# A hybrid encoder step on one core: W_out prepared by ScalarE and GpSimd, the last head pair's mask added by TensorE, its cached keys stacked one step sooner

## The chip, the core and the metric

The kernel runs on one core of a Trainium2 chip. The core has five instruction streams that matter here: TensorE (PE in the profile, with its weight loads shown apart as PEld), VectorE (DVE), ScalarE (ACT), GpSimd (POOL) and SyncE (SP), which only issues DMA transfers. Each stream runs its instructions in order; streams wait for one another by semaphores. The metric is the device time of one execution in microseconds.

## The reference, cut to what matters

The reference computes one layer of an encoder for a prompt of 1024 frames and for a sample of 64 further frames, whose 512 earlier frames lie in a cache. A combined projection of x feeds three groups of heads: six forgetting-attention heads (fox), four channel groups of a spatial-gating MLP (sgu), and six stick-breaking heads (sb). The head outputs are normalised per head, multiplied by a gain `g_mix`, and go through one output projection `w_out`; then come a layer norm, an MLP of 4096 hidden columns and a second layer norm.

What the change touches is the stick-breaking attention and the gain with the output projection:

```python
z = jnp.einsum('bqhd,bkhd->bhqk', q, k).astype(jnp.float32) / math.sqrt(D_HEAD)
mask = kpos[None, :] < qpos[:, None]
log_rem = jnp.where(mask, jax.nn.log_sigmoid(-z), 0.0)
after = lax.cumsum(log_rem, axis=3, reverse=True) - log_rem
a = jnp.where(mask, jnp.exp(jax.nn.log_sigmoid(z) + after), 0.0)
...
oh = oh * lax.rsqrt(jnp.mean(oh * oh, axis=-1, keepdims=True) + RMS_EPS)
o = (oh.reshape(B, T, D_MIX) * g_mix).astype(o_sgu.dtype)
return jnp.einsum('bte,ed->btd', o, w_out)
```

The kernel takes the weight of a key as sigmoid(z) times the product of sigmoid(-z) over the keys between it and the query.

## The kernel before

**Numbers in two parts.** A matrix operand is kept as a rounded high part (type fp32r) and the rest, its low part. ACT makes the high part with a copy that rounds; a subtraction (`lo_sub`, L97) makes the low part on DVE or POOL. A product is three matmuls, high by high, high by low, low by high (`PASSES`).

**The stage with the change.** Two generators are traced in turns by a loop with hand-set costs: `fill` (projections) and `attn` (attention). `attn` runs over six head pairs (three fox, then sb 0, 1, 2; the last is `pairs[5]`). For each pair it takes four steps u of 256 queries, each for two heads h, and then the sample. A step is `Unit.a_steps` (scores and weights) and `Unit.b_steps` (transposes of the weights, their split in two parts, the product with the values). `fill` meanwhile makes the next pair's keys, values and queries; beside the last pair it makes the gate `u` of the sgu group (`sgu_u`), and then the first two tiles of the output projection (`mix`, L244). A scheduler under the kernel fixes each engine's order from readiness in its own model and the order of the trace, so that an instruction can run well ahead of its place in the program.

- **Scores** (`qk_rows`, L554): into a PSUM bank of tag s, of which there are two. On the diagonal block of 128 keys DVE adds the mask `m_fox` or `m_sb` (L561, 128 x 128). For sb two sigmoids on ACT follow (L536, L537), a scan of products on DVE from the last key to the first (L538, up to 1024 columns), and a product on POOL (L540). PE transposes the result (L602, ptsb), ACT and DVE split it (L570 and L97, pthsb), PE multiplies by the values (L612 to L615, osb), ACT copies the result out (L625, osbsb), PE transposes it into the one bank of tag tr (L633, otpsb), and DVE adds up two halves (L634).
- **The sample's cache** (`Sample`): `load` at u = 1 fetches keys and values by DMA; `prep_steps`, traced at u = 3, transposes the keys in two rounds through the tr bank (L671, pkcsb), and `k_stack` copies each head's part on ACT (L441) and takes the low part on DVE (L97), both into kc_sb; POOL makes the values' parts (L676, L97, vc_sb). `a_steps` then multiplies (L692, Ss0sb). The two kc tiles are of tag kp, which has ten buffers; the pair's four key tiles and the five partial sums `up` of `sgu_u` have the same tag.
- **W_out** (`load_wo`, sixteen calls of 128 x 512, named xT<-rwo in the profile): a DMA (L970) puts a piece into a raw tile (tag vp, ten buffers, or raw, two). ACT writes piece x gain, rounded, into the high part (L973), and DVE writes piece x gain - high into the low part (L974). The parts lie in the memory of `xT`, the transposed input, so that each piece waits until the projections have read that part of xT. `sgu_u` calls them from its tile 4 on.
- **sgu_u** (L355, sgu<-wu,xT): for nine tiles and two halves of the depth, into one of two acc banks. The first half is copied out by ACT (L853, up), the second added by DVE (L856), then the gelu goes over ACT, DVE (L752), ACT and POOL (L754), and a DMA stores it to u_dr.
- **mix**: `prep` loads a tile of head outputs (oo, from o_dr) and of u_dr (uu), POOL multiplies (L183), ACT squares (L185), DVE sums and scales (L187, L192); the tile is transposed (L200) and split (oTb), and 48 matmuls (L244, mx) follow.

The SP queue issues all these DMAs in one order: raw pieces of weights, query copies (L115), stores to o_dr and u_dr, loads of oo and uu.

Of the kernel before, what the change touches and what calls it, by code (L numbers as in the profile page):

```python
# [12 lines left out]
F32 = mybir.dt.float32  # L13
F32R = mybir.dt.float32r
AF = mybir.ActivationFunctionType
ALU = mybir.AluOpType
# [4 lines left out]
P = 128  # L21
# [15 lines left out]
BIG = 1e30  # L37
# [19 lines left out]
def _build(nc, tc, a, es):  # L57
# [23 lines left out]
    ident = cp.tile([P, P], F32, name="ident")  # L81
# [14 lines left out]
    def lo_sub(eng, out, src, hi):  # L96
        eng.tensor_tensor(out, src, hi.bitcast(F32), op=ALU.subtract)  # L97
# [22 lines left out]
    wo = []  # L120
# [161 lines left out]
    gmx = sp.tile([P, KT], F32, name="gmx")  # L282
    with ExitStack() as p1:
        sa = p1.enter_context(tc.tile_pool(name="sa", bufs=1, side="right"))
# [4 lines left out]
        def mask(name, base, fill):  # L289
            m = sp.tile([P, P], F32, name=name + "_f", tag="gl", bufs=3)  # L290
            nc.gpsimd.memset(m, 0.0)
            nc.gpsimd.affine_select(m, m, pattern=[[-1, P]], compare_op=ALU.is_ge,
                                    fill=fill, base=base, channel_multiplier=1)
            r = sp.tile([P, P], F32R, name=name)
            nc.vector.tensor_copy(r, m)
            return r

        m_fox = mask("m_fox", 0, BIG)
        m_sb = mask("m_sb", -1, -BIG)

# [239 lines left out]
            nc.gpsimd.tensor_tensor(s[:, 0:n - 1], s[:, 0:n - 1], g[:, 1:n], op=ALU.mult)  # L540
            return s

        def qk_rows(nm, qd, h, half, nk, kp, msk):
            chunks = []
            eng = {"dve": nc.vector, "pool": nc.gpsimd, "pe": nc.tensor}['dve' if msk is m_fox else 'dve']
            on_pe = eng is nc.tensor
            for c0 in range(0, nk, 512):
                w = min(512, nk - c0)
                sps = ps.tile([P, 512], F32, name=f"S{nm}_{c0}", tag="s", bufs=2)
                for b0 in range(c0, c0 + w, 256):  # L550
                    n = min(256, nk - b0)
                    last = b0 + n == nk
                    for s in range(2):
                        nc.tensor.matmul(sps[:, b0 - c0:b0 - c0 + n], qd[:, h, s, half * P:(half + 1) * P],  # L554
                                         kp[b0 // 256][:, h, 0:n], start=(s == 0), stop=(s == 1 and not (last and on_pe)))
                    if last and on_pe:
                        nc.tensor.matmul(sps[:, w - P:w], identr, msk, start=False, stop=True)
                    elif last:
                        d = sps[:, w - P:w]
                        if eng is nc.vector:  # L560
                            nc.vector.tensor_tensor(d, d, msk.bitcast(F32), op=ALU.add)  # L561
                        else:
                            nc.gpsimd.affine_select(d, d, pattern=[[-1, P]], compare_op=ALU.is_ge,
                                                    fill=BIG if msk is m_fox else -BIG,
                                                    base=0 if msk is m_fox else -1, channel_multiplier=1)
                chunks.append((c0, w, sps[:, 0:w]))
            return chunks

# [4 lines left out]
        class Unit:  # L573
# [4 lines left out]
            def a_steps(self):  # L578
                st, u, h = self.st, self.u, self.h
                for half in range(2):  # L580
                    i = 2 * u + half
                    nk = (i + 1) * P
                    k2 = f"{st['nm']}_{i}_{h}"
                    ch = qk_rows(k2, st["qd"][u], h, half, nk, st["kp"], m_fox if st["fox"] else m_sb)
                    if st["fox"]:
                        hh = 2 * st["hp"] + h
                        self.rows.append(softmax_rows(k2, ch, st["cb"][h], nk, lsum[:, i, hh:hh + 1]))
                    else:
                        self.rows.append(stick_rows(k2, ch, nk))
                    yield 0.109 * (i + 2)  # L590
# [281 lines left out]
        pairs = []  # L872
        for fox, hp in ((True, 2), (True, 1), (True, 0), (False, 0), (False, 1), (False, 2)):
# [3 lines left out]
                fox=fox, hp=hp, first=first, quick=len(pairs) in (0, 1, 5), nm=pre + str(hp), nv=262 if first else 256,  # L877
                scale=-0.125 if fox else 0.125, qd={}, kp=[], vp=[],
# [85 lines left out]
        def load_wo(i, half, q):  # L964

            k = 4 * i + q
            cs = slice(half * 512, (half + 1) * 512)
            raw = (sa.tile([P, 512], F32, name=f"rwo{k}_{half}", tag="vp", bufs=10) if (2 * k + half) % 3
                   else sp.tile([P, 512], F32, name=f"rwo{k}_{half}", tag="raw", bufs=2))
            nc.sync.dma_start(raw, w_out[:, k, cs])  # L970
            hi = wo[i][0][:, q, cs]
            g = gmx[:, k:k + 1]
            nc.scalar.activation(hi, raw, AF.Copy, scale=g)  # L973
            nc.vector.scalar_tensor_tensor(wo[i][1][:, q, cs], raw, g, hi.bitcast(F32),  # L974
                                           op0=ALU.mult, op1=ALU.subtract)

        cur = {"j": 0}

        def attn():
            seq = []  # L980
            for j, st in enumerate(pairs):
                for u in range(4):
                    for h in range(2):
                        seq.append((j, u, h, Unit(st, u, h)))
                seq.append((j, 4, 0, Sample(st)))

            def a_of(x):
                j, u, h, un = x
                cur["j"] = j
                st = pairs[j]  # L990
                if u < 4:
                    if u == 0 and h == 0:
                        if j == 5:
                            yield (5, "kv")
                        st["smp"] = seq[[i for i, y in enumerate(seq) if y[0] == j and y[1] == 4][0]][3]
                    yield (j, u)
                    if u == 0 and h == 0:
                        if j == 0:
                            yield (0, "c0")
                        if st["fox"]:  # L1000
                            st["cb"] = []
                            for hh in range(2):
                                cb = sp.tile([P, TP], F32, name=f"cb{st['nm']}_{hh}", tag="row", bufs=ROWS)
                                r = 2 * st["hp"] + hh
                                nc.sync.dma_start(cb, bcast(c_dr[r:r + 1, 0:TP]))
                                st["cb"].append(cb)
                    if u == 1 and h == 0:
                        st["smp"].load()
                    if u == 3 and h == 0:
                        yield from st["smp"].prep_steps()  # L1010
                if j == 0 and u == 4:
                    yield (0, "c1")
                yield from un.a_steps()
                if u < 4 and h == 1:
                    live["qd"] -= 1

            settled = set()

            def settle(x):
                c_pend.extend(c_list)  # L1020
                c_list.clear()
                if x[:3] in settled:
                    return
                settled.add(x[:3])
                if x[1] == 3 and x[2] == 1:
                    live["kp"] -= 4
                if x[1] == 4:
                    live["kn"] -= 1

            nxt = a_of(seq[0])  # L1030
            yield from nxt
            for i, x in enumerate(seq):
                b = x[3].b_steps()
                nxt = a_of(seq[i + 1]) if i + 1 < len(seq) else iter(())
                alive = [nxt, b]
                k = 0
                while alive:
                    g = alive[k % len(alive)]
                    try:
                        c = next(g)  # L1040
                    except StopIteration:
                        alive.remove(g)
                        continue
                    if isinstance(c, tuple) and c not in done:
                        for cb_ in b:
                            yield cb_
                        settle(x)
                    yield c
                    k += 1
                    if k == 2 and c_pend:  # L1050
                        while c_pend:
                            c_pend.pop(0)()
                settle(x)
            while c_pend:
                c_pend.pop(0)()
# [392 lines left out]
    with p3:  # L1448
# [100 lines left out]
        with in_order(border):  # L1549
            raw = up_load(2)  # L1550
            ch = chain(1, 0)
# [25 lines left out]
        ch = chain(NP - 3, 1)  # L1577
        for i in range(7):
            ch.product(i)
        ch = chain(NP - 3, 0)  # L1580
# [82 lines left out]
    with ExitStack() as p3:  # L1663
# [290 lines left out]
        g = 2 * c  # L1954
# [135 lines left out]
```

## Time and profile before

| | |
|---|---|
| runs shown | 1410.02, 1411.81, 1411.91 us; median 1411.81 |
| the profiled execution's own time | 1411.73 us |
| its span, first to last instruction | 1410.0 us |
| granted TensorE clock, mean | 0.980 |
| PE busy | 1328.1 us, 8827 matmuls |
| DVE, ACT, POOL busy | 1002.6, 718.5, 602.3 us |

The page of the profile has the busy time of each engine, the span in 40 slices with the busy share of each engine in tenths, the chain that ended last, and groups of equal instructions. A group's row gives line, engine, operation, the tile written and those read with shapes, then busy time, mean duration in ns, and the idle time of its engine just before with what ended it. A row of the waits says who waited for whom: total us, times, longest. A row of the order in time gives start, duration, engine, line and operation. A row of stretches gives the stretch, its length, the busy time of each engine with its instructions, the granted clock, the share of DMA and its GB/s; asked for one line alone it shows that line's engine only.

### The profile page before, as it was taken

How to read it: one execution, taken by the hardware profiler on the slowest of the kernel's cores; microseconds unless marked ns; L12 is line 12 of the kernel's file. 1: busy time of each engine (PE TensorE's matmuls, PEld its weight loads, DVE VectorE, ACT ScalarE, POOL GpSimd, SP SyncE). 2: the span in 40 equal slices, each digit the busy share in tenths (PEclk: the TensorE clock that was granted, in tenths of full speed). 3: DMA queues.
4: the chain of work that ended last, by engine and by line, in shares of the span. 5: the costliest groups of instructions: out<-in, count | busy, mean ns of one | idle time of the engine just before them, and what ended most of it. 6: DMA issues, size and time to landing. Idle time of an engine off the chain costs nothing.

```text
span 1410.0 us, 24288 instructions
## 1 busy us (share of the span) xinstructions
PE 1328.1 (94%) x8827; PEld 1206.8 (86%) x8827; DVE 1002.6 (71%) x1799; ACT 718.5 (51%) x1561; POOL 602.3 (43%) x663
## 2 busy tenths in 40 slices
PE   7999999999989997999989999999979999999996
PEld 6899999999888986866889999999967787777774
DVE  3577565676786599887866768767678777667777
ACT  3366565666665485333423323232247667667675
POOL 3222222266565535654411122212166665654657
PEclk9999999999999998999999999999999999999999
DMA  7324242322313434422234434344558344344343
GB/s 218 77 78 113 58 117 65 81 63 56 80 27 83 127 91 135 132 105 68 76 110 140 153 133 139 117 166 139 173 187 295 99 160 165 118 136 150 101 135 128
DMA packets 149217, 168.87 MB, mean 120 GB/s; under 512 B 27100, under 2 KB 115484, under 8 KB 149096
## 3 DMA queue, kind: packets, MB, share of 16 engines
q1 hardware_dynamic: 149096, 167.30, 37.9%
q8 instruction: 70, 1.15, 0.3%
q14 instruction: 51, 0.42, 0.1%
HBM read 109.26 MB, written 51.71 MB: 114 GB/s over the span
## 4 chain that ended last, share of the span: by engine, by line
PE 63%; DVE 12%; ACT 7%; DMA 6%; POOL 6%; issue 5%; SPq 1%; DVEq 0%; ACTq 0%; POOLq 0%
PE zA L1264 9%; PE A L1715 6%; PE zD L1264 6%; PE mx L244 5%; PE kvsb L355 5%; PE kvfox L355 4%; PE D L1715 3%; PE zC L1264 3%; PE zB L1264 3%; DVE snsb L538 2%; DMA raw<-w_in 2%; PE qfox L496 2%; PE Sfox L554 2%; DMA rd<-w_down 2%; PE ptfox L602 1%
## 5 line engine op out<-in xcount | busy, mean ns | idle before, releaser
L97 POOL TENSOR_TENSOR wa<-wr,wa 128x512 fp32r<-128x512 f32 x42 | 63.8, 1548 | 228.5 <-ACT wa L1204 228.5
L97 POOL TENSOR_TENSOR wd<-rd,wd 128x512 fp32r<-128x512 f32 x77 | 101.1, 1322 | 121.2 <-ACT wd L1204 116.9
L244 PE MATMUL mx<-xT,oTb 128*128 128x512 f32 (+1 forms) x416 | 108.0, 412 | 1.6 <-ACT oTb L202 1.5
L1264 PE MATMUL zD<-xo,ws 128*128 128x288 f32 (+1 forms) x720 | 98.1, 289 | 0.6 <-DVE h4a L1426 0.3
L1264 PE MATMUL zA<-xo,ws 128*128 128x288 f32 (+1 forms) x720 | 98.1, 290 | 0.0
L244 PEld LDWEIGHTS mx<-xT,oTb 128*128 128x128 f32 (+1 forms) x416 | 78.1, 193 | 21.7 <-ACT oTb L202 2.5
L1264 PEld LDWEIGHTS zD<-xo,ws 128*128 128x128 f32 x720 | 93.7, 189 | 1.1 <-DVE h4a L1426 0.5
L1264 PEld LDWEIGHTS zA<-xo,ws 128*128 128x128 f32 x720 | 94.1, 189 | 0.1
L540 POOL TENSOR_TENSOR sgsb<-sgsb,snsb 128x127 f32<-128x127 f32 (+7 forms) x48 | 58.8, 1227 | 78.8 <-DVE snsb L538 64.3
L355 PE MATMUL kvfox<-wkvfox,xT 128*128 128x256 f32 (+3 forms) x624 | 90.6, 294 | 1.5 <-ACT wkvfox L331 0.5
L1204 ACT ACTIVATE wd<-rd 128x512 fp32r<-128x512 f32 x105 | 63.8, 624 | 51.6 <-DMA rd<-w_down 25.8
L355 PE MATMUL kvsb<-wkvsb,xT 128*128 128x256 f32 (+1 forms) x624 | 87.7, 286 | 0.0
L1715 PE MATMUL A<-wd,wd 128*128 128x512 f32 x312 | 83.0, 401 | 2.5 <-DVE acc L1682 2.3
L355 PEld LDWEIGHTS kvfox<-wkvfox,xT 128*128 128x128 f32 (+1 forms) x624 | 81.6, 193 | 3.3 <-DVE xT L97 1.0
L1396 POOL TENSOR_TENSOR rd<-rd 128x512 f32<-128x512 f32 x56 | 78.9, 1409 | 10.9 <-DVE b L97 8.7
L538 DVE TENSOR_TENSOR_SCAN snsb<-snsb,one 128x128 f32<-128x128 f32 (+7 forms) x48 | 72.2, 1507 | 13.3 <-ACT snsb L537 12.5
L1275 ACT ACTIVATE sn<-zA 128x256 f32<-128x256 f32 (+1 forms) x80 | 31.0, 390 | 98.4 <-PE zA L1264 82.6
L355 PEld LDWEIGHTS kvsb<-wkvsb,xT 128*128 128x128 f32 (+1 forms) x624 | 79.2, 187 | 0.2
L1715 PEld LDWEIGHTS A<-wd,wd 128*128 128x128 f32 x312 | 58.9, 191 | 18.9 <-DVE acc L1682 4.2
L1715 PE MATMUL A<-wd,h4a 128*128 128x512 f32 x240 | 65.1, 395 | 0.4 <-DVE acc L1682 0.3
L1478 ACT ACTIVATE ws<-wr 128x1024 fp32r<-128x1024 f32 x28 | 29.0, 1057 | 54.0 <-DVE wr L1214 54.0
L1715 PEld LDWEIGHTS A<-wd,h4a 128*128 128x128 f32 x240 | 44.5, 188 | 12.6 <-ACT p L1732 1.2
(537 smaller groups left out, 3746.2 us busy)
## 6 DMA issues: line engine op xcount, KB each, us to landing
h_dr<-hh SPq DMA_DIRECT2D x30, 512.0 KB, 3.2
rd<-w_down SPq DMA_DIRECT2D x30, 512.0 KB, 4.5
awa<-h_dr SPq DMA_DIRECT2D x30, 512.0 KB, 4.5
wr<-w_up SPq DMA_DIRECT2D x14, 1024.0 KB, 5.4
hr<-h_dr SPq DMA_DIRECT2D x32, 384.0 KB, 3.6
h_dr<-hh SPq DMA_DIRECT2D x30, 384.0 KB, 3.9
raw<-w_in SPq DMA_DIRECT2D x44, 256.0 KB, 3.3
xr<-x_prompt SPq DMA_DIRECT2D x8, 512.0 KB, 7.2
```

Source lines behind the costliest of these rows:

```text
L97: eng.tensor_tensor(out, src, hi.bitcast(F32), op=ALU.subtract)
L244: nc.tensor.matmul(acc[0:m], oT[:, k, hx, 0:m], wo[k // 4][hw][:, k % 4, cs], start=(i == 0), stop=(i == len(seq) - 1))
L355: nc.tensor.matmul(acc[0:n, c0:c0 + n1 - n0], xT[k // 4][:, k % 4, c:c + n], wt[:, k, hw, n0:n1], start=(i == 0), stop=(i == len(seq) - 1))
L496: nc.tensor.matmul(acc[:, 0:w], wq[:, k, hw, :], xT[k // 4][:, k % 4, c:c + w], start=(i == 0), stop=(i == len(seq) - 1))
L538: nc.vector.tensor_tensor_scan(g[:, 0:n][:, ::-1], g[:, 0:n][:, ::-1], one.broadcast_to([P, n]), 1.0, op0=ALU.mult, op1=ALU.bypass)
L540: nc.gpsimd.tensor_tensor(s[:, 0:n - 1], s[:, 0:n - 1], g[:, 1:n], op=ALU.mult)
L1204: nc.scalar.activation(hi, raw, AF.Copy)
L1264: nc.tensor.matmul(z, w[:, hw, k], xop(s, bo, hx)[:, k, :], start=(new and k == 0 and j == 0), stop=(k == 3 and j == 2), skip_group_check= ...
L1275: nc.scalar.activation(c, z, AF.Copy)
L1396: eng.tensor_tensor(r[:, o], r[:, x], r[:, y], op=ALU.subtract)
L1478: nc.scalar.activation(ws[:, 0, q, c], src[:, q], AF.Copy)
L1715: nc.tensor.matmul(z, h[:, hx, q, o], wset[self.c % 2][q][:, hw, wb], start=((n in (0, 3) or n == 1 and self.c == 0) and q == 0 and j == 0 ...
```

## The change

It has three parts and one helper tile. (1) `load_wo`: the gain is multiplied into the raw tile in place by ACT, a second ACT copy rounds it into the high part, and POOL makes the low part with `lo_sub`; DVE has no part in it. (2) `qk_rows` has an argument `on_pe`, set for the last pair alone: there the mask is added in PSUM by a further matmul, of a rounded identity `identr` with the mask, and DVE does not touch the scores. `identr` is made by one DVE copy at the start. (3) The sample's `prep_steps` of the last pair (j = 5) is traced at u = 2 instead of u = 3. Code that no path used goes with it.

```diff
--- before.py
+++ after.py
@@ -295,6 +295,8 @@
             nc.vector.tensor_copy(r, m)
             return r
 
+        identr = sa.tile([P, P], F32R, name="identr")
+        nc.vector.tensor_copy(identr, ident)
         m_fox = mask("m_fox", 0, BIG)
         m_sb = mask("m_sb", -1, -BIG)
 
@@ -540,10 +542,8 @@
             nc.gpsimd.tensor_tensor(s[:, 0:n - 1], s[:, 0:n - 1], g[:, 1:n], op=ALU.mult)
             return s
 
-        def qk_rows(nm, qd, h, half, nk, kp, msk):
+        def qk_rows(nm, qd, h, half, nk, kp, msk, on_pe=False):
             chunks = []
-            eng = {"dve": nc.vector, "pool": nc.gpsimd, "pe": nc.tensor}['dve' if msk is m_fox else 'dve']
-            on_pe = eng is nc.tensor
             for c0 in range(0, nk, 512):
                 w = min(512, nk - c0)
                 sps = ps.tile([P, 512], F32, name=f"S{nm}_{c0}", tag="s", bufs=2)
@@ -557,12 +557,7 @@
                         nc.tensor.matmul(sps[:, w - P:w], identr, msk, start=False, stop=True)
                     elif last:
                         d = sps[:, w - P:w]
-                        if eng is nc.vector:
-                            nc.vector.tensor_tensor(d, d, msk.bitcast(F32), op=ALU.add)
-                        else:
-                            nc.gpsimd.affine_select(d, d, pattern=[[-1, P]], compare_op=ALU.is_ge,
-                                                    fill=BIG if msk is m_fox else -BIG,
-                                                    base=0 if msk is m_fox else -1, channel_multiplier=1)
+                        nc.vector.tensor_tensor(d, d, msk.bitcast(F32), op=ALU.add)
                 chunks.append((c0, w, sps[:, 0:w]))
             return chunks
 
@@ -581,7 +576,8 @@
                     i = 2 * u + half
                     nk = (i + 1) * P
                     k2 = f"{st['nm']}_{i}_{h}"
-                    ch = qk_rows(k2, st["qd"][u], h, half, nk, st["kp"], m_fox if st["fox"] else m_sb)
+                    ch = qk_rows(k2, st["qd"][u], h, half, nk, st["kp"], m_fox if st["fox"] else m_sb,
+                                 st is pairs[5])
                     if st["fox"]:
                         hh = 2 * st["hp"] + h
                         self.rows.append(softmax_rows(k2, ch, st["cb"][h], nk, lsum[:, i, hh:hh + 1]))
@@ -969,10 +965,9 @@
                    else sp.tile([P, 512], F32, name=f"rwo{k}_{half}", tag="raw", bufs=2))
             nc.sync.dma_start(raw, w_out[:, k, cs])
             hi = wo[i][0][:, q, cs]
-            g = gmx[:, k:k + 1]
-            nc.scalar.activation(hi, raw, AF.Copy, scale=g)
-            nc.vector.scalar_tensor_tensor(wo[i][1][:, q, cs], raw, g, hi.bitcast(F32),
-                                           op0=ALU.mult, op1=ALU.subtract)
+            nc.scalar.activation(raw, raw, AF.Copy, scale=gmx[:, k:k + 1])
+            nc.scalar.activation(hi, raw, AF.Copy)
+            lo_sub(nc.gpsimd, wo[i][1][:, q, cs], raw, hi)
 
         cur = {"j": 0}
 
@@ -1006,7 +1001,7 @@
                                 st["cb"].append(cb)
                     if u == 1 and h == 0:
                         st["smp"].load()
-                    if u == 3 and h == 0:
+                    if u == (2 if j == 5 else 3) and h == 0:
                         yield from st["smp"].prep_steps()
                 if j == 0 and u == 4:
                     yield (0, "c1")
```

## The prediction

> **What bounds the kernel now.** The page first: which engine is full, and where.
>
> ```profile
> span 1410.0 us, 24288 instructions
> ...
> PE 1328.1 (94%) x8827; PEld 1206.8 (86%) x8827; DVE 1002.6 (71%) x1799; ACT 718.5 (51%) x1561; POOL 602.3 (43%) x663
> ...
> PE   7999999999989997999989999999979999999996
> ...
> DVE  3577565676786599887866768767678777667777
> ```
>
> PE is the bound over the whole, so only time in which PE stands still can be won. A slice is 35.25 us; in the 15th and 16th (493 to 564 us) DVE is at 9 tenths, and in the 16th PE falls to 7. The edits lie there, from the last stick-breaking pair's scores (477 us) to the first output-projection matmul (558.5 us). The table by stretches:
>
> ```profile
> 477.00:558.50 81.50, 68.74 (x518) 65.55 (x516) 74.76 (x114) 57.97 (x142) 40.37 (x42) 0.94 0.42 126
> ...
> 500.00:558.50 58.50, 48.06 (x354) 45.73 (x353) 55.28 (x79) 40.84 (x95) 25.95 (x23) 0.91 0.38 117
> ...
> 560.00:580.00 20.00, 19.64 (x104) 16.11 (x103) 17.39 (x36) 7.06 (x15) 16.25 (x17) 1.00 0.39 126
> 580.00:600.00 20.00, 20.00 (x94) 16.16 (x93) 13.95 (x23) 6.38 (x10) 12.12 (x13) 1.00 0.46 140
> 600.00:616.00 16.00, 16.00 (x79) 12.41 (x78) 11.90 (x20) 5.78 (x10) 7.17 (x12) 1.00 0.27 99
> ```
>
> Columns: stretch, length, busy PE, PEld, DVE, ACT, POOL, then granted clock. In 477 to 558.5 PE idles 81.50 - 68.74 = 12.8 us while DVE is busy 74.76 of 81.5; from 500 on DVE is at 94.5% and the clock is 0.91, a further 48.06 x 0.09 = 4.3 us. From 560 to 616 PE is full, so what is won before 558.5 arrives at the end unless something later waits on a fixed time, and I see nothing such. Who holds PE there, by the waits (total us, times, longest):
>
> ```profile
> PE Ss0sb L692 <- DVE kc_sb L97: 3.7, 1, 3.7
> PE osb L614 <- DVE pthsb L97: 3.4, 3, 1.8
> PE Ssb L554 <- ACT snsb L537: 1.9, 2, 1.6
> ...
> ACT sgsb L536 <- DVE Ssb L561: 9.6, 6, 2.3
> ```
>
> DVE's order in time shows what stands ahead of those it keeps waiting:
>
> ```profile
> 512.09 1.40 DVE L974 SCALAR_TENSOR_TENSOR xT<-rwo,gmx,xT 128x512 fp32r<-128x512 f32 x2
> 513.41 1.27 DVE L97 TENSOR_TENSOR pthsb<-ptsb,pthsb 128x512 fp32r<-128x512 f32 x2
> ...
> 527.81 3.13 DVE L974 SCALAR_TENSOR_TENSOR xT<-rwo,gmx,xT 128x512 fp32r<-128x512 f32 x2
> 530.86 0.28 DVE L561 TENSOR_TENSOR Ssb<-Ssb,m_sb 128x128 f32<-128x128 f32 x1
> ...
> 542.30 2.21 DVE L752 SCALAR_TENSOR_TENSOR g1u<-g1u,up 128x256 f32<-128x256 f32 x1
> 544.43 1.80 DVE L974 SCALAR_TENSOR_TENSOR xT<-rwo,gmx,xT 128x512 fp32r<-128x512 f32 x2
> 546.26 0.42 DVE L97 TENSOR_TENSOR kc_sb<-pkcsb,kc_sb 64x256 fp32r<-64x256 f32 x1
> ...
> 547.05 0.75 DVE L974 SCALAR_TENSOR_TENSOR xT<-rwo,gmx,xT 128x512 fp32r<-128x512 f32 x1
> 547.71 1.15 DVE L97 TENSOR_TENSOR pthsb<-ptsb,pthsb 128x512 fp32r<-128x512 f32 x2
> ```
>
> L974 makes the low parts of W_out, which nobody needs before 558.5. Yet the split of the probabilities (pthsb) comes behind it at 512 and 547, the mask L561 at 530.9 comes behind 3.13 us of it, and the cached keys' low part (kc_sb) at 546.26. So 3.7 + 3.4 + 1.6 (the longer wait of Ssb, by way of mask and sigmoid) = **8.7 us** of PE's 12.8 idle stand behind L974, L561 or a late kc_sb.
>
> **The change, part by part.** The rows of what goes and of the nearest to what comes:
>
> ```profile
> L974 DVE SCALAR_TENSOR_TENSOR xT<-rwo,gmx,xT 128x512 fp32r<-128x512 f32 x16 | 15.5, 995 | 0.7 <-ACT xT L973 0.7
> ...
> L561 DVE TENSOR_TENSOR Ssb<-Ssb,m_sb 128x128 f32<-128x128 f32 x15 | 4.4, 294 | 3.8 <-PE Ssb L554 3.5
> ...
> L973 ACT ACTIVATE xT<-rwo,gmx 128x512 fp32r<-128x512 f32 x16 | 10.8, 731 | 0.0
> ...
> L331 ACT ACTIVATE wu<-raw 128x512 fp32r<-128x512 f32 x4 | 2.4, 624 | 0.0
> ...
> L97 POOL TENSOR_TENSOR wu<-raw,wu 128x512 fp32r<-128x512 f32 x4 | 5.2, 1294 | 0.3 <-ACT wu L331 0.3
> ...
> L554 PE MATMUL Ssb<-kpsb,qdsb 128*128 128x128 f32 x14 | 2.6, 269 | 0.3 <-ACT snsb L537 0.3
> ```
>
> Edit 1, W_out: DVE loses 16 L974, 15.5 us. ACT keeps 16 scalings at 0.73 us (now in place) and gains 16 plain copies at 0.624 = 10.0 us. POOL gains 16 subtractions at 1.294 = 20.7 us. The scaling no longer writes xT, so it need not wait until the projection has read xT. Behind each subtraction on POOL stand the stick-breaking products (L540) and the gelu products (L754), for which transposes and stores wait. The raw tile comes free after POOL instead of DVE, and the SP queue already stands for that:
>
> ```profile
> SPq L970 <- DVE xT L974: 8.6, 7, 3.7
> ...
> L970 SPq DMA_DIRECT2D rwo<-w_out x16: 327/330/537, 473.5 to 531.8; - x16
> ```
>
> The 16 loads are the same; behind a waiting one on SP stand stores to o_dr and u_dr and the loads of uu and oo for the first projection tile. I cost this at nothing: POOL has 58.5 - 25.95 = 32.6 us idle after 500. Without that cover it is a subtraction for each of the seven waits, 7 x (1.294 - 0.995) = 2.1 us.
>
> Edit 2, masks: DVE loses 16 x 0.294 = 4.7 us (15 of them in the stretch); ACT's sigmoid follows PE directly, so its 9.6 us of waiting for masks go. PE gains 16 matmuls of 128 columns in fp32r. That operation (ident by mask, whole) is not in the trace; one of 128 columns in a row of others:
>
> ```profile
> 492.47 0.22 PE L613 MATMUL osb<-pthsb,vpsb 128*128 128x128 f32 x1
> 492.53 0.28 PE L614 MATMUL osb<-pthsb,vpsb 128*128 128x128 f32 x1
> 492.64 0.33 PE L615 MATMUL osb<-pthsb,vpsb 128*128 128x256 f32 x1
> ```
>
> L613 and L614 take 0.17 us from start to start for two (0.09 each), and the 128-column form of L554 lasts 0.269 us in the mean, overlaps counted: 16 x 0.09 = 1.4 to 16 x 0.269 = 4.3 us. Nothing can be gained below zero, since it is added work. I take 0.12 us, near the first, because the mask follows two matmuls of its own group: **1.9 us**. The copy identr is one DVE cast at the start, where DVE still waits for the first x; 0.2 us without that cover.
>
> Edit 3, cache keys: four transposes, four ACT copies, four DVE subtractions move from u = 3 to u = 2, one step of the pair earlier. No DMA moves, since the load stays at u = 1, and the values' parts on POOL ran early already:
>
> ```profile
> L97 POOL TENSOR_TENSOR vc_sb<-cache_sb_v,vc_sb x12: 451/457/464, 320.9 to 477.0; 128x128 fp32r<-128x128 f32 x12
> ```
>
> The last of twelve ran at 477.0, some 70 us ahead of the key's low part at 546.26. The 3.7 us wait goes. The four keys still take the one tr bank, for which the output transposes of the finished heads wait, but one step sooner, in DVE's company of fewer instructions; I cost that at nothing. The copies may wait for a buffer (first rival).
>
> What is late next: ACT. In the stretch it rises to 57.97 + 10.0 = 68.0 us. After 500 it has 40.84 + 10.0, less the scalings of the first six tiles, which can run before 500 (six, an estimate: the buffers that tags vp and raw have free by the code): 6 x 0.73 = 4.4. That is 46.4 us of some 53, 12% free, where DVE has 5.5% free now. New waits on ACT lie between nothing and the 8.7 us that DVE causes. If waits go as the inverse of the free share, 8.7 x 5.5 / 12 = 4.0 us; counting only the 5.0 that edit 3 does not move, 2.3 us. I take **3.0**. The clock recovers with the idle time: (8.7 - 3.0) / 12.8 x 4.3 = 1.9 us.
>
> Sum: -8.7 + 3.0 + 1.9 - 1.9 = **-5.7 us**. The profiled execution took 1411.73 us, 1.73 more than its span, and the median of the runs shown is 1411.81, so the one stands for the other: 1411.7 - 5.7 = **1406.0**.
>
> [...] The trace shows POOL and DVE standing in each other's way:
>
> ```profile
> L974 DVE SCALAR_TENSOR_TENSOR xT<-rwo,gmx,xT x16: 721/740/2464, 500.3 to 547.0; 128x512 fp32r<-128x512 f32 x16
> ...
> 541.88 2.35 POOL L540 TENSOR_TENSOR sgsb<-sgsb,snsb 128x1023 f32<-128x1023 f32 x1 [2.29 <-PE sgu L355]
> ```
>
> L752 began at 542.30, within this POOL instruction, lasted 2.21 us and ended at 544.51, just after POOL at 544.23; L974 ranges from 0.72 to 2.46 us. Its 16 cost 15.5 - 16 x 0.72 = 4.0 us beyond their least. [...]
>
> ```profile
> 477.00:558.50 81.50, 25.96 (x16) 0.94 0.42 126
> ```
>
> [...]
>
> **The rivals.** (a) *Buffers for the cache keys.* Tag kp has ten: four hold the pair's keys, five the projection's partial sums (up), one is left until a sum is used up. Two key tiles taken sooner leave the ninth tile's sum without one until then.
>
> ```profile
> L853 ACT ACTIVATE up<-sgu x9: 360/391/445, 489.8 to 513.3; 128x256 f32<-128x256 f32 x8, 64x256 f32<-64x256 f32 x1
> ...
> 522.74 1.74 POOL L754 TENSOR_TENSOR sguu<-g1u,up 128x256 f32<-128x256 f32 x2
> ```
>
> It was stored at 513.3; the first sum is used up at 524.5. For 11 us one of two acc banks would be held, and some four projection tiles (an estimate) would each wait for their emptying, 0.42 us as kc_sb takes and one pthsb ahead of it on DVE, 1.27 / 2: 4 x 1.06 = 4.2 us, so **1410.2**. Against: another pair's buffers come free meanwhile. Chance 0.11. (b) *ACT becomes what DVE was*, all 8.7 us remain and the masks are added: **1413.6**. For: 12% free. Against: ACT loses its 9.6 us of waiting. 0.05. (c) *Edit 3 changes nothing*, because the order on PE stays as it was: -5.7 + 3.7 + 1.2 of the clock = **1410.9**; against it, the values' parts already run ahead of their place. 0.02. [...] 0.14.
>
> **How the numbers follow.** Forecast 0.68, (a) to (c) 0.18, (d) 0.14. A measurement of this kernel can tell about 0.2%, 2.8 us: the forecast is faster by more, (a) to (c) lie within it, (d) beyond it. Low end: no new wait on ACT and the clock with it, -8.7 + 1.9 - 2.9 = -9.7, and half of the other 4.1 us of idle time: 1400. High end: (b), 1414. Outside stay (d) and a little of the forecast's tail.
>
> **What would show it.** L974 gone from DVE, DVE under 75% in the stretch; no wait of S0 on kc_sb and none of the sigmoid on a mask; the first mx matmul near 553 instead of 558.5, and the same distance from there to the end. Wrong would be: PE waiting on ACT or POOL for 9 us or more; the 16 scans taking far more than 25.96 us; acc waiting for up.

## The result, and the profile after

The changed kernel takes 1417.84 us (median of 7 runs, 1414.58 to 1420.25), beside 1411.81 for the kernel before on the same chip: ratio **1.0044, 95% interval [1.0029, 1.0058]**. It is slower, by about 6 us, where 1406.0 was predicted. (Of all runs below one, of the kernel with fills, took 1470.18 us at a clock of 0.841; it is left out.) The profiled execution took 1417.84 us, its span 1415.8. The page of the profile after:

```profile
span 1415.8 us, 24280 instructions
...
PE 1333.2 (94%) x8843; PEld 1214.3 (86%) x8843; DVE 994.2 (70%) x1768; ACT 728.7 (51%) x1577; POOL 633.5 (45%) x679
...
PE   7899999999989987999989999999988999999996
```

PE has 16 matmuls more; its 16th slice still stands at 7 tenths, and the 15th has fallen from 9 to 8. The table by stretches after (length, busy PE, PEld, DVE, ACT, POOL, granted clock):

```profile
477.00:558.50 81.50, 71.48 (x552) 68.08 (x551) 59.97 (x81) 65.47 (x155) 67.89 (x59) 0.96 0.45 136
500.00:558.50 58.50, 49.74 (x377) 46.87 (x375) 44.14 (x58) 46.56 (x107) 50.85 (x38) 0.94 0.39 120
560.00:580.00 20.00, 17.84 (x84) 14.61 (x84) 12.55 (x24) 8.13 (x19) 11.31 (x14) 0.83 0.32 101
```

VectorE fell as forecast, from 55.28 to 44.14 of 58.5 us. GpSimd doubled, from 25.95 to 50.85: it is now at 87%, the fullest engine of the stretch. And the stretch from 560 to 580, nearly full at clock 1.00 before, has idle time and clock 0.83. Who holds PE, by the waits from 477 to 600 us:

```profile
PE ptsb L598 <- POOL sgsb L542: 3.1, 2, 2.2
PE op L200 <- issue: 2.9, 1, 2.9
PE otpsb L629 <- ACT osbsb L621: 1.9, 1, 1.9
PE Ssb L554 <- ACT snsb L539: 1.4, 2, 1.0
PE sgu L357 <- DVE up L852: 1.4, 1, 1.4
PE osb L610 <- DVE pthsb L97: 1.3, 2, 1.1
```

The wait of S0 on kc_sb is gone, and that on pthsb fell from 3.4 to 1.3. In their place PE waits for GpSimd's stick products (3.1) and, before the first transposes of the first output-projection tile (op), for 2.9 us. That last wait was there before too, but shorter, and the tile's first powers (L190) came at 552.76:

```profile
PE op L200 <- DVE oo L192: 1.3, 1, 1.3
...
552.76 1.66 POOL L190 TENSOR_TENSOR ss<-ss,negh 128x8 f32<-128x8 f32 x1 [0.53 <-ACT osbsb L625]
```

GpSimd's order in time after the change shows what stands ahead of that tile's head products (L183) and powers:

```profile
544.51 5.40 POOL L97 TENSOR_TENSOR xT<-rwo,xT 128x512 fp32r<-128x512 f32 x4
549.88 0.87 POOL L183 TENSOR_TENSOR oo<-oo,uu 128x128 f32<-128x128 f32 x2
550.71 0.73 POOL L750 TENSOR_TENSOR sguu<-g1u,up 128x256 f32<-128x256 f32 x1
551.40 0.86 POOL L183 TENSOR_TENSOR oo<-oo,uu 128x128 f32<-128x128 f32 x2
552.23 3.74 POOL L97 TENSOR_TENSOR xT<-rwo,xT 128x512 fp32r<-128x512 f32 x3
555.94 0.72 POOL L750 TENSOR_TENSOR sguu<-g1u,up 128x256 f32<-128x256 f32 x1
556.62 1.65 POOL L190 TENSOR_TENSOR ss<-ss,negh 128x8 f32<-128x8 f32 x1
558.26 1.26 POOL L97 TENSOR_TENSOR xT<-rwo,xT 128x512 fp32r<-128x512 f32 x1
559.48 1.64 POOL L190 TENSOR_TENSOR ss<-ss,negh 128x8 f32<-128x8 f32 x1
```

From 544.5 to 561.1 GpSimd never rests, and 10.4 us of it are W_out's low parts. They are not the whole of the wait: the first powers were done at 558.27, but the scaling by them (L192), after which PE could go on, stood behind other reductions on VectorE, one of which waited for ScalarE's square:

```profile
559.84 0.69 DVE L187 TENSOR_REDUCE ss<-sq 128x8 f32<-128x512 f32 x1 [0.30 <-ACT sq L185]
560.45 0.68 DVE L192 TENSOR_TENSOR oo<-oo,ss 128x512 f32<-128x512 f32 x1
```

On PE, in the same order of time:

```profile
558.09 0.28 PE L611 MATMUL osb<-pthsb,vpsb 128*128 128x256 f32 x1
561.23 1.09 PE L200 MATMUL op<-ident,oo 128*128 128x128 f32 x4 [2.85 <-issue]
563.24 0.79 PE L244 MATMUL mx<-xT,oTb 128*128 128x512 f32 x1 [0.93 <-ACT oTb L202]
```

The first mx matmul comes at 563.24; it was at 558.53 before, and 553 was forecast. The gap costs twice. By stretches of 1 us around it:

```profile
558.50:559.50 1.00, 0.00 (x0) 0.00 (x0) 0.96 (x2) 0.58 (x2) 1.00 (x2) 1.00 0.00 0
559.50:560.50 1.00, 0.00 (x0) 0.00 (x0) 0.70 (x3) 0.62 (x2) 1.00 (x2) 0.89 0.00 0
560.50:561.50 1.00, 0.27 (x2) 0.30 (x3) 1.00 (x3) 0.00 (x0) 1.00 (x2) 0.50 0.00 0
...
566.50:567.50 1.00, 1.00 (x5) 0.81 (x4) 0.09 (x1) 0.17 (x1) 0.73 (x1) 0.69 0.39 126
567.50:568.50 1.00, 1.00 (x6) 0.82 (x5) 0.43 (x1) 0.51 (x2) 0.00 (x0) 1.00 0.35 118
```

After the gap PE works at half clock until 567: about 6.8 us at 0.50, from 560.3 to 567.1. Nine mx matmuls took 3.76 us there (563.24 to 567, 0.42 us each), and twelve took 2.40 us at clock 1.00 (567.5 to 569.9, 0.20 us each). PE was busy for 4.9 of the 6.8 us, so about 2.5 us were lost.

This one profile must not be read as the whole loss. Of the 5.8 us between the two spans, 2.8 had come about by the first matmul of the stick-breaking keys and values (kvsb, at 218.6 us before and 221.4 after), where the engines run the instructions of the kernel before in the same order (but for the copy identr): up to there the clock stood at 0.50 for 3.4 us before and for 10.2 us after. From run to run the mean clock differs too, from 0.974 to 0.982 in 114 runs of the kernel before. Counted from that matmul, the tile's first powers come 1.1 us later than before, the first transposes 1.3, the first mx matmul 1.9, and the end 3.0. So the size is taken from all runs: each has a span and a mean granted clock, and span x (1 - clock) is what the clock costs if PE has work throughout the dips, an upper bound. The rest is work and idle time.

### The profile page after: what moved, and what is told of

Same layout as the page of the kernel before. It is cut to its first block, busy times and chain, and to the rows that moved or that the text cites. A ratio compares the mean times of both kernels' runs of the same rounds, so it can differ in the third digit from the quotient of the medians.

```text
span 1415.8 us, 24280 instructions
## 1 busy us (share of the span) xinstructions
PE 1333.2 (94%) x8843; PEld 1214.3 (86%) x8843; DVE 994.2 (70%) x1768; ACT 728.7 (51%) x1577; POOL 633.5 (45%) x679
## 4 chain that ended last, share of the span: by engine, by line
PE 55%; DVE 12%; POOL 9%; DMA 9%; ACT 7%; issue 6%; SPq 1%; ACTq 0%; DVEq 0%; POOLq 0%
PE zA L1259 9%; PE zD L1259 6%; PE kvsb L357 4%; PE A L1710 4%; PE kvfox L357 4%; PE zC L1259 3%; PE zB L1259 3%; DMA rd<-w_down 3%; PE D L1710 2%; PE qfox L498 2%; PE mx L244 2%; PE Sfox L554 2%; POOL wd L97 2%; DVE snsb L540 1%; PE ptfox L598 1%
## 5 line engine op out<-in xcount | busy, mean ns | idle before, releaser
L542 POOL TENSOR_TENSOR sgsb<-sgsb,snsb 128x127 f32<-128x127 f32 (+7 forms) x48 | 63.2, 1321 | 59.3 <-DVE snsb L540 51.6
L540 DVE TENSOR_TENSOR_SCAN snsb<-snsb,one 128x128 f32<-128x128 f32 (+7 forms) x48 | 75.2, 1571 | 18.3 <-ACT snsb L539 17.8
L1259 PE MATMUL zA<-xo,wa 128*128 128x288 f32 (+1 forms) x360 | 51.2, 295 | 4.1 <-ACT wa L1199 3.4
```

Of the source, the lines that this page charges most:

```text
L540: nc.vector.tensor_tensor_scan(g[:, 0:n][:, ::-1], g[:, 0:n][:, ::-1], one.broadcast_to([P, n]), 1.0, op0=ALU.mult, op1=ALU.bypass)
L1259: nc.tensor.matmul(z, w[:, hw, k], xop(s, bo, hx)[:, k, :], start=(new and k == 0 and j == 0), stop=(k == 3 and j == 2), skip_group_check= ...
```

## The experiments

Each kernel was timed beside the kernel before on the same chip. In the table, "span" is the difference of the mean span to that of 114 runs of the kernel before (1409.4 us), "clock" the part of it in span x (1 - clock) (29.8 us before; the standard error of such a difference is 0.6 to 1.8 us), "rest" what is left, and "GpSimd" its busy time in 500 to 558.5 us by the profile.

| kernel | ratio [95%] | span | clock | rest | GpSimd |
|---|---|---|---|---|---|
| the whole change | 1.0044 [1.0029, 1.0058] | +6.2 | +3.6 | +2.6 | 50.85 |
| edit 1 alone | 1.0052 [1.0034, 1.0069] | +8.0 | +3.0 | +4.9 | 49.23 |
| edit 2 alone | 0.9989 [0.9972, 1.0007] | -0.6 | -0.4 | -0.1 | 29.35 |
| edit 3 alone | 1.0019 [1.0005, 1.0033] | +3.4 | -1.3 | +4.7 | 29.86 |
| edits 2 and 3 | 0.9994 [0.9979, 1.0009] | -0.1 | +1.2 | -1.3 | 29.22 |
| edit 1, low parts on VectorE | 1.0049 [1.0031, 1.0067] | +6.4 | +1.2 | +5.2 | 28.20 |
| edit 1, first 8 on GpSimd | 1.0035 [1.0020, 1.0051] | +5.4 | +1.2 | +4.2 | 39.66 |
| edit 1, last 8 on GpSimd | 1.0071 [1.0056, 1.0086] | +9.4 | +6.1 | +3.2 | 39.88 |
| edit 1, scaled by VectorE | 1.0063 [1.0042, 1.0083] | +8.5 | +7.8 | +0.7 | 47.62 |
| before + ScalarE pass | 1.0050 [1.0031, 1.0068] | +6.4 | +1.8 | +4.6 | 26.76 |
| before + GpSimd subtraction | 1.0084 [1.0062, 1.0105] | +11.8 | +9.1 | +2.8 | 48.19 |
| before + GpSimd fills | 1.0051 [1.0033, 1.0069] | +6.7 | +5.3 | +1.4 | 48.41 |
| whole, low parts on VectorE | 1.0009 [0.9995, 1.0023] | +1.2 | -0.3 | +1.5 | 24.82 |
| whole, scaled by VectorE | 1.0047 [1.0030, 1.0064] | +6.3 | +2.8 | +3.6 | 49.02 |
| whole, first 8 on GpSimd | 0.9997 [0.9984, 1.0010] | -0.7 | +0.4 | -1.1 | 42.89 |
| whole, last 8 on GpSimd | 0.9999 [0.9983, 1.0014] | -0.8 | -1.3 | +0.5 | 32.42 |
| whole, last 8 as before | 1.0011 [0.9991, 1.0031] | +1.2 | -2.3 | +3.5 | 41.85 |

**The three edits alone, and edits 2 and 3 together.** The theory after the result was that GpSimd's queue carries the loss (Q); the rivals were the cache keys' buffers (B) and the masks on PE (P). Each edit is its part of the diff above. Edit 1 alone:

> Edit 1 alone: W_out scaled in place on ScalarE, low parts on GpSimd; mask and keys as before. Theory Q (GpSimd's queue: the 16 subtractions stand ahead of the stick-breaking products and of the head products and powers of the first projection tile, so PE waits there): this edit carries the loss, 1416 to 1421 us, with PE or ScalarE waiting on GpSimd for 3 us or more before the first mx matmul. Rival B (the cache keys taken sooner leave the projection's sums without a buffer): this edit without that one gains, 1405 to 1411.

Edit 2 alone:

> Edit 2 alone: the last pair's mask by a matmul. Theory Q and rival B: within 3 us of before, 1409 to 1413 (4.7 us off VectorE, some 2 us on PE). Rival P (the masks on PE are the loss): 1415 or more.

Edit 3 alone:

> Edit 3 alone: the last pair's cached keys stacked at u = 2. Theory Q: 1408 to 1412. Rival B: 1415 or more, with the copies of up spread out to 525 or later instead of ending at 513.

Edits 2 and 3:

> Edits 2 and 3 without 1. Theory Q: 1405 to 1411, faster than before. Rival B or P: 1415 or more.

Edit 1 alone has the whole loss, so it is the edit to take apart. Edits 2 and 3 together are worth nothing that can be measured, although PE waits for stick products in that kernel as long as in the whole change:

```profile
PE ptsb L598 <- POOL sgsb L542: 3.1, 1, 3.1
```

So this wait alone does not make the loss. Edit 3 alone loses 3.4 us, which Q had not expected. The row of the gate's partial sums (up), which share ten buffers with the cache keys, shows what it changes: first and last copy start at 489.8 and 513.3 us before, and with edit 3 alone

```profile
L853 ACT ACTIVATE up<-sgu x9: 360/380/400, 490.5 to 526.9; 128x256 f32<-128x256 f32 x8, 64x256 f32<-64x256 f32 x1
```

The last sum is copied out 13.6 us later, and PE waits for it:

```profile
PE sgu L355 <- DVE up L856: 3.3, 1, 3.3
```

That is the mechanism of the prediction's rival (a), and its price of 4.2 us is near the 3.4 measured. But edits 2 and 3 together lose nothing, and their sums are just as late:

```profile
L849 ACT ACTIVATE up<-sgu x9: 363/379/393, 489.8 to 528.0; 128x256 f32<-128x256 f32 x8, 64x256 f32<-64x256 f32 x1
```

So the lateness is shown; that it is what costs edit 3 alone its 3.4 us is not.

**Is it GpSimd at all?** Edit 1 with the low parts on VectorE, and with half of them there:

```diff
-            lo_sub(nc.gpsimd, wo[i][1][:, q, cs], raw, hi)
+            lo_sub(nc.vector, wo[i][1][:, q, cs], raw, hi)
```

> Edit 1 with one difference: W_out is scaled in place and copied by ScalarE as in the change, but the 16 low parts are made by a subtraction on VectorE, none on GpSimd. So ScalarE has its 16 further passes of about 0.7 us (some 10 us), GpSimd has nothing new, and VectorE keeps 16 passes of about 1 us. Theory Q (GpSimd's in-order queue and what waits for it is the cost): the loss of edit 1 alone (1419.0 us) goes; within 3 us of the kernel before on the same chip, 1409 to 1415, with no burst of four subtractions ahead of the head products. Rival A (the second pass on ScalarE is the cost, through a later up, later evictions and a later transpose of the attention's result): the loss stays, 1417 us or more. A tie-breaker: if the low part waits one step longer for two ScalarE passes and that matters, PE's waits on VectorE in 500 to 558 us grow.

First 8 on GpSimd (`nc.gpsimd if i == 0 else nc.vector`):

> Edit 1 with the low parts of the first 8 pieces (first half of the columns' groups) on GpSimd and of the other 8 on VectorE. Theory Q, if the loss comes from the subtractions that stand ahead of the stick products of the last pairs: most of the 6.5 us of edit 1 alone stays, 1415 to 1420. If it comes from those ahead of the first projection tile's head products and powers: it goes, 1409 to 1414. The rival A (ScalarE's second pass) expects the same as edit 1 alone, 1417 to 1421, for this and its mirror image alike.

The mirror image:

> The mirror image: the first 8 pieces' low parts on VectorE, the other 8 on GpSimd. Theory Q, if the loss comes from the subtractions ahead of the first projection tile's head products and powers (after about 535 us): 1415 to 1420. If it comes from those ahead of the last pairs' stick products: 1409 to 1414. Both halves at about +3 us would say that the loss is spread over both places. Rival A: 1417 to 1421 as for its mirror image.

The whole change with the low parts on VectorE:

> The whole change, but with the low parts by a subtraction on VectorE. Theory Q: the 5 to 6 us that the whole change lost go; edits 2 and 3 together measured 1410.8, so 1408 to 1414. Rival A (ScalarE): 1416 or more, as the whole change. Rival L (not the queue: the loss needs GpSimd and VectorE together in the memory of the SBUF, so that VectorE's scans stretch): as Q, 1408 to 1414; what tells L from Q here is the length of VectorE's scans of 128x768 elements, which L expects back at about 1.7 us and which take 2.85 us in the changed kernel.

Theory Q fell for edit 1 alone: without one subtraction on GpSimd it still loses 6.4 us, and both halves lose too, nearly as the rival A (ScalarE's second pass) had it. They are not alike, however: the last 8 on GpSimd lose 4.0 us more than the first 8 (standard error 1.3), all of it in the clock. So here the place seems to matter, and no run shows why. The PE waits of the kernel with all low parts on VectorE name VectorE:

```profile
PE osb L614 <- DVE pthsb L97: 7.2, 3, 5.4
```

But in the whole change the same move takes most of the loss away, from +6.2 to +1.2 us. So there are two costs: ScalarE's second pass, which edits 2 and 3 nearly cover, and GpSimd's subtractions, about 5 us, which they do not cover.

**Each cost by itself, added to the kernel before.** ScalarE's pass made twice, and a subtraction on GpSimd that nobody reads:

```diff
             nc.scalar.activation(hi, raw, AF.Copy, scale=g)
+            nc.scalar.activation(hi, raw, AF.Copy, scale=g)
```

> The kernel before with one suspected cost added by itself: ScalarE makes each of the 16 high parts of W_out twice (the same pass of about 0.7 us again, onto the same tile), everything else as before; GpSimd has nothing new and VectorE's pass waits for the second of the two, as in edit 1. Theory A (the second pass on ScalarE, some 10 us in the stretch from 479 to 555 us, is what edit 1 alone costs; suggested by edit 1 with the low parts on VectorE, which lost 6 us too): 1415 to 1421 us. Theory Q (GpSimd's queue): within 3 us of before, 1409 to 1414.

```diff
+            nc.gpsimd.tensor_tensor(raw, raw, hi.bitcast(F32), op=ALU.subtract)
```

> The kernel before with the other suspected cost added by itself: after VectorE's low part, GpSimd subtracts the high part from the raw piece once more, in place, 16 times; nothing reads the result, and only the buffer of the raw piece comes free later. So GpSimd has the 16 subtractions of the change in its queue, and VectorE and ScalarE have what they had. Theory A: within 3 us of before, 1409 to 1414. Theory Q: 1415 to 1421, with stick products, head products or powers late behind bursts of subtractions. If both this and the doubled ScalarE pass lose, the stretch has no room on either engine and each theory holds half.

Edit 1 and the whole change with the scaling on VectorE, so that ScalarE has one pass as before:

```diff
-            nc.scalar.activation(raw, raw, AF.Copy, scale=gmx[:, k:k + 1])
+            nc.vector.tensor_scalar(raw, raw, gmx[:, k:k + 1], None, op0=ALU.mult)
```

> Edit 1 with the scaling in place made by VectorE (a multiplication by the gain, an estimate of 0.4 to 0.75 us a piece from the rows of 128x512 on VectorE) in place of ScalarE's; ScalarE has one pass a piece as before, GpSimd makes the low parts as in the change. Theory A: the loss of edit 1 goes, 1408 to 1414. Theory Q: it stays, 1415 to 1421.

> The whole change with the scaling in place made by VectorE; GpSimd makes the low parts as in the change. The whole change with the low parts on VectorE was within 2 us of before, so with edits 2 and 3 in place it is GpSimd that costs. Theory Q: 1414 to 1420, as the whole change. Theory A: 1408 to 1413.

Both costs are real: +6.4 us from 16 passes on ScalarE, +11.8 from 16 subtractions on GpSimd. They do not add: edit 1 alone has both, and loses 8.0. With ScalarE relieved, and 16 multiplications on VectorE instead, both versions still lose (+8.5 and +6.3), as Q had it. The two kinds of loss look different in the table: ScalarE's pass is paid in the rest (4.6 and 5.2 of 6.4 us), GpSimd's more in clock (9.1 of 11.8, 7.8 of 8.5; but 3.6 of 6.2 and 2.8 of 6.3 with edits 2 and 3).

**Is it the queue alone?** Fills write the SBUF but read nothing of it:

```diff
+            for _ in range(3):
+                nc.gpsimd.memset(raw, 0.0)
```

> The kernel before with work added to GpSimd that writes the SBUF but reads nothing from it: after VectorE's low part, three fills of each of the 16 raw pieces (dead by then). From the profile's row of a 128x128 fill (0.20 us) three of 128x512 are an estimated 1.5 us a piece, about what one subtraction took on GpSimd. Like the added subtraction (which lost 12 us) they stand in GpSimd's queue ahead of stick products, and wait for VectorE's low part first. Theory Q (the queue is the cost): 1417 to 1424. [...]

The fills took 0.525 us each, 23.0 us in the stretch by the first of these rows, with a scan and the low parts on VectorE below it:

```profile
L977 POOL MEMSET rwo<- 128x512 f32 x47 | 23.0, 525 | 3.1 <-DVE xT L974 2.7
...
L974 DVE SCALAR_TENSOR_TENSOR xT<-rwo,gmx,xT 128x512 fp32r<-128x512 f32 x16 | 17.1, 1100 | 0.8 <-ACT xT L973 0.7
...
L538 DVE TENSOR_TENSOR_SCAN snsb<-snsb,one 128x768 f32<-128x768 f32 x2 | 3.5, 1744 | 0.0
```

The same two groups with the added subtraction:

```profile
L974 DVE SCALAR_TENSOR_TENSOR xT<-rwo,gmx,xT 128x512 fp32r<-128x512 f32 x16 | 20.5, 1315 | 0.7 <-ACT xT L973 0.7
...
L538 DVE TENSOR_TENSOR_SCAN snsb<-snsb,one 128x768 f32<-128x768 f32 x2 | 4.0, 1987 | 0.0
```

With fills the 768-column scan lasts 1.744 us, as in the kernel before (1.744 there too); the subtraction stretches it to 1.987. All 16 scans took 26.0 us before, 26.7 with the fills and 27.7 with the subtraction, and L974 took 15.5, 17.1 and 20.5. So the subtraction lengthens VectorE's instructions more than the fills do, though the fills do not leave them unchanged. Yet the fills alone lose 6.7 us. So time in GpSimd's queue is enough, together with the raw piece that comes free behind it: the SP queue waits 21.2 us for it with the fills and 21.8 with the subtraction, beside 8.6 before. (Edits 2 and 3 together have 26.0 us of that wait, and lose nothing.) Of the subtraction's 11.8 us some 5 are more than the fills cost (standard error 1.4); no run shows whether they come from the longer instructions on VectorE.

**Which of the sixteen?** In the whole change, half of the low parts on each engine:

> The whole change with the low parts of the first 8 pieces on GpSimd and of the other 8 on VectorE. All on GpSimd lost 6 us, all on VectorE 2 us. If each subtraction on GpSimd costs the same, about 1415 us. If only those late in the stretch cost (near the first projection tile), 1410 to 1414; if only the early ones (beside the scans of 768 and 640 columns), 1415 to 1419.

> The mirror image of the half: the whole change with the first 8 low parts on VectorE and the last 8 on GpSimd. Theory Q as it now stands (only subtractions that stand in GpSimd's queue ahead of the first projection tile's head products and powers cost, by a gap on PE of about 3 us before the first transposes of that tile and a halved clock after it): most of the whole change's loss, 1414 to 1419, with PE's transposes of the first tile waiting at their start. Rival N (it is the number on GpSimd that counts, eight are free wherever they stand): as the half, 1409 to 1413.

Neither half loses anything. With the first 8 on GpSimd the scans beside them are stretched just as in the whole change. The row of the 768-column scans with all 16 on GpSimd:

```profile
L540 DVE TENSOR_TENSOR_SCAN snsb<-snsb,one 128x768 f32<-128x768 f32 x2 | 5.9, 2940 | 1.8 <-ACT snsb L539 1.8
```

and with the first 8 there:

```profile
L540 DVE TENSOR_TENSOR_SCAN snsb<-snsb,one 128x768 f32<-128x768 f32 x2 | 5.9, 2946 | 1.8 <-ACT snsb L539 1.8
```

So those stretched scans cost nothing at the end. In that kernel the first tile's transposes follow at 557.83 with no wait of PE:

```profile
557.62 0.41 PE L611 MATMUL osb<-pthsb,vpsb 128*128 128x256 f32 x1
557.83 0.95 PE L200 MATMUL op<-ident,oo 128*128 128x128 f32 x4
```

But the mirror image, with the 8 that stand ahead of that tile on GpSimd, loses nothing either. My theory that the place alone decides fell, and its rival, the amount, held for kernels with edits 2 and 3. In the last column of the table, among these: GpSimd at 24.8 to 42.9 of 58.5 us loses nothing measurable, at 49.0 and 50.9 it loses 6 us. If its share of the stretch is what decides, the bound lies somewhere between 73% and 84%; no run stood there.

**A mixture.** Edits 2 and 3, the first 8 pieces as in the change, the last 8 as before:

> Edits 2 and 3 whole; of W_out the first 8 pieces as in the change (scaled in place, copied, low part on GpSimd) and the last 8 as in the kernel before (one pass on ScalarE, low part on VectorE). Against the half it saves ScalarE 8 passes of about 0.65 us and costs VectorE 8 times some 0.1 us. Theory: at or under the half, 1406 to 1411; it would be the best of the mixtures if ScalarE's passes still cost anything with edits 2 and 3 in place. Rival (ScalarE's passes are covered there): equal to the half, 1409 to 1413.

1.0011 [0.9991, 1.0031]: ScalarE's saved passes bring nothing once edits 2 and 3 are in. No version here is faster than the kernel before beyond its interval.

## Why the prediction was wrong, point by point

- **What bounds the kernel: right.** L974 is gone from VectorE, VectorE stands at 44.14 / 58.5 = 75%, and of the 8.7 us the 3.7 on kc_sb went whole, 2.1 of the 3.4 on pthsb and 0.5 on the scores (1.9 to 1.4). But PE's idle time in 477 to 558.5 us fell only from 12.8 to 10.0 us, since other waits came in their place.
- **Edit 1, the step that failed:** "I cost this at nothing: POOL has 58.5 - 25.95 = 32.6 us idle after 500." The sum of idle time was taken as cover for a queue, so the 16 subtractions on GpSimd entered the sum as zero, where they cost about 5 us. The 16 subtractions took 25.7 us, not 20.7:

```profile
L97 POOL TENSOR_TENSOR xT<-rwo,xT 128x512 fp32r<-128x512 f32 x16 | 25.7, 1635 | 0.0
...
L968 ACT ACTIVATE rwo<-rwo,gmx 128x512 f32<-128x512 f32 x16 | 11.4, 721 | 4.4 <-DMA rwo<-w_out 4.2
...
L969 ACT ACTIVATE xT<-rwo 128x512 fp32r<-128x512 f32 x16 | 9.0, 625 | 0.0
...
L557 PE MATMUL Ssb<-m_sb,identr 128*128 128x128 f32 x16 | 4.1, 255 | 0.0
```

  They came in bursts, three of them of four subtractions and 5.4 to 8.9 us, ahead of stick products and head products; the products were named as standing "behind each subtraction" and then not priced. The runs put about 5 us on it (+6.2 with all 16 on GpSimd, +1.2 with none; standard error 1.2). The uncovered price of 2.1 us was only that of the raw tile's release, which rose from 8.6 to 10.0 us, within that bound (to 27.0 in edit 1 alone).
- **What is late next: the wrong engine.** ACT's added time was right (11.4 + 9.0 - 10.8 = 9.6 against 10.0), and 1.2 us, less than 3.0, is all that the change loses with GpSimd out of it. GpSimd was not asked in that step, although by the same arithmetic it stood at 25.95 + 20.7 = 46.7 of 58.5 us, 80%, beside ACT's 46.4 of some 53.
- **Edit 2: within its bounds, at the high end.** 16 x 0.255 = 4.1 us of PE by the last row above, against 1.9 taken and 4.3 as bound. Alone it is -0.6 us of span, within what can be told from nothing; the 4.7 us that left VectorE were no gain by themselves. The copy identr took 0.44 us, not 0.2.
- **Edit 3: no gain.** The 3.7 us wait went, but alone the edit loses 3.4 us, with rival (a)'s late sums, to which I gave 0.11. With edit 2 beside it the sums are as late and nothing is lost, so in the whole change this rival is not shown to cost anything.
- **The clock: the wrong sign.** -1.9 was forecast from idle time; the runs have +3.6 +/- 1.2, at face value over half of the loss. That the clock recovers in proportion to PE's idle time was an estimate that no run shows: in 500 to 558.5 us it stood at 0.94 beside 8.8 us of PE's idle time (before, 0.91 beside 10.4), in 560 to 580 at 0.83 beside 2.2 us (before, 1.00 beside 0.4).
- **The rivals.** The result lies on the slow side, beyond the 2.8 us that a measurement can tell, where the forecast has (d) with 0.14. No run shows longer scans on VectorE to be the cause. The scans took

```profile
477.00:558.50 81.50, 30.24 (x17) 0.96 0.45 136
```

  against 25.96 for 16 before. The 17th is short: the two scans of 128 columns take 1.2 us here, where 0.3 us of them lay in the stretch before. So the scans came to about 3.3 us more; and the kernel with the first 8 low parts on GpSimd keeps 2.4 us of it (5.9 against 3.5 for its 768-column scans) and loses nothing.

What stays open: through which wait of PE the 16 subtractions cost their 5 us, for the waits of single profiles do not add up to it, and the scheduler orders each of these kernels anew. How much of it is the queue and how much longer instructions on VectorE other than the scans: the whole change was not run with fills. Why ScalarE's second pass costs 6 us without edits 2 and 3 and about 1 us with them: VectorE's share would fit two kernels (55.88 of 58.5 us in edit 1 with the low parts on VectorE, 52.05 in the whole change with them there), but not the kernel before with ScalarE's pass added, which loses as much at 54.47, under the 55.28 of the kernel before. Nor was it tried where between 43 and 49 us of GpSimd the loss begins.

## What to carry to other kernels

The sum of an engine's idle time does not show that added work is covered: GpSimd had 32.6 us of it in 500 to 558.5 us, and 16 subtractions of 25.7 us cost about 5 us. Before moving instructions to an engine, list what stands next in its queue in the busiest stretch, and add its new total as a share of that stretch, for every engine that receives work. Move part of the work first: here, with edits 2 and 3 in place, 8 of 16 subtractions were free and 16 cost about 5 us. Take the size from several runs with their clocks, for one profile of each kernel differs from the next by as much as this change is worth.

## What the runs showed of the hardware

The clock's dips came in whole steps of 3.4 us: in the stretches of half a microsecond from 470 to 700 us of all 18 profiles, it fell to exactly 0.50 for 3.4, 6.8 or 10.2 us, once for 17.1, after stretches of some 4 us in which PE idled 1.0 to 4.0 us. In the gap of 2.85 us above, the clock fell 1.9 us after the end of PE's last matmul, and in the wait of 1.9 us for osbsb 1.3 us after. The length of a gap does not settle it: in the whole change with the last 8 on GpSimd PE idled 1.9 us from 552 and again from 556 us, and the clock stayed at 1.00:

```profile
552.00:553.00 1.00, 0.00 (x0) 0.00 (x0) 1.00 (x3) 1.00 (x4) 1.00 (x2) 1.00 1.02 332
553.00:554.00 1.00, 0.12 (x1) 0.12 (x2) 1.00 (x2) 1.00 (x4) 1.00 (x1) 1.00 0.88 324
...
556.00:557.00 1.00, 0.00 (x0) 0.00 (x0) 0.97 (x2) 1.00 (x3) 1.00 (x2) 1.00 0.00 0
557.00:558.00 1.00, 0.05 (x1) 0.05 (x1) 1.00 (x4) 0.60 (x2) 1.00 (x2) 1.00 0.00 0
558.00:559.00 1.00, 1.00 (x8) 0.92 (x8) 1.00 (x2) 0.07 (x1) 1.00 (x1) 1.00 0.00 0
```

By the rates of the mx matmuls above, a step of 3.4 us at 0.50 takes at most 3.4 x 0.5 = 1.7 us of PE's time. In the 114 runs of the kernel before, span x (1 - clock) ranged from 25.3 to 36.7 us and the time from 1404.70 to 1417.83 us.
